# First results copied into the FFN accumulator, x loaded within the first up set, and turns ahead of the narrow block, in a two-layer hybrid decoder trunk

## The chip, the core and the metric

The kernel runs on one core of a Trainium2 chip. Five engines work side by side, each on its own queue of instructions in order: TensorE (PE: matmuls, with weight loads as PEld), VectorE (DVE), ScalarE (ACT), GpSimd (POOL) and SyncE (SP). DMAs are issued from the queues of SP, ACT and POOL. The metric is the time of one execution on the device in microseconds (us). The median of 3 runs of the kernel before is 2119.82 us (2116.66 to 2121.93).

## What is computed

Two layers of a hybrid decoder trunk over 512 tokens of width 1024, in float32. A layer is a mixer (four branches, each lifted and gated, summed, one output projection) and then the part that the change touches, a SwiGLU FFN with an inner width of 2816:

```python
for l in range(DEPTH):                      # 2 layers
    x = x + merged @ w_out                  # the mixer's end
    hf = rmsnorm(x, norm_ffn)
    gate, up = jnp.split(hf @ ffn_w_up, 2, axis=-1)
    x = x + (jax.nn.silu(gate) * up) @ ffn_w_down
```

## The kernel before

**Precision.** Each float32 operand is split in a high half (rounded, `hi`) and the rest (`lo`), and a product is three matmuls, hi·hi, hi·lo, lo·hi (`mm3`, lines 280 to 285). Weights come by DMA on SP's queue into raw buffers; ScalarE writes the high half (`w_hi`, through the helper `A`, so all of ScalarE's work has line 99), VectorE the low half (`w_lo`, line 1099 in `split`, line 236 in `Chunk`).

**Raw buffers.** `raw_tile` (line 1083) hands out buffers of 1 MB: two of `w_raw` and, every third time, the single `w_raw7`. A buffer is used again, in the order in which the program asks for it, only when its last reader is done. The profile names both `w_raw`.

**The FFN.** 2816 inner columns are eleven groups of 256. Ten of them go through a scheme with seven products in place of eight (Strassen's, in Winograd's form), two groups of 256 at a time in an *up set*; the eleventh, group 10, is the *narrow block*, computed plainly in two halves of 128 columns (`up_plain`). The scheme needs sums of blocks of the weights. Those are not computed on an engine: `weight_sums` (line 1104) has GpSimd issue DMAs that copy one block in DRAM and add others to it, each waiting for the one before ("one by one", line 1110). Layer 0's are started early in its mixer, layer 1's at the end of layer 0's FFN (line 1075). They end in DRAM as `up_sums` and `w_sums`, from where SP loads them as raw weights.

**Parts.** Each layer's FFN has three parts (lines 1390 to 1427). A part first makes inner columns, then multiplies them down into the accumulator `acc` (512 tokens by 1024):

- part 0: up set 0 and the narrow block, then `down` over groups 0, 1, 10;
- part 1: up sets 1 and 2, then `down` over groups 2 to 5;
- part 2: up sets 3 and 4, then `down` over groups 6 to 9. In layer 0 the last two groups go through `add_down` (line 1059) instead, which adds `acc` and x as well and writes the next layer's input.

**An up set** (`up_set`, line 1310) has seven products, each of 24 matmuls on one raw buffer, named after the left operand: A11, A12, S2, S1, S3, S4, A22, in this order. Left operands S1 to S4 are sums of quarters of the normalized input `h`, made once per layer by `left_sums` (line 1246), which uses the buffer `acc` as its scratch; S1 alone stands in `h1`, a buffer of the kind `a_hi`/`a_lo`, of which there are four (`N_OPS`); S2 to S4 stand in `hs`. The results, `v` and `u`, are evicted between products. In part 0, `between` (the first half of the narrow block, its result turned and kept in `fy`) stands after A12. S2's weights take the third turn of the raw buffers and S4's the sixth, both `w_raw7` in layer 1.

**Operands.** The inner columns have to be turned (tokens to the free axis) before they can be multiplied down: `turned` (line 1377) makes four 128x128 transposes on TensorE against the identity (line 1380) and a copy on ScalarE. `operands` (line 1147) then makes, from two turned tiles, the quarters and their sums as hi/lo pairs. `pairs_of` (line 1385) does so for an up set's two groups.

**The order in part 0.** After the up set comes the second half of the narrow block (`up_plain(1, ...)`), then `pairs_of` for the set, then two copies on ScalarE that put `h1` into a quarter of `h` that is read no more after the narrow block (this frees the buffer of `h1` for a fourth operand; `where[S1]` then points there), then `acc`, and last the operand of group 10. In layer 0 `acc` is cleared by a memset on GpSimd (line 1405). In layer 1, the last, `acc` starts as x: `x_in` (line 1283) loads half of x from `x_spill` into `w_raw7`, turns 16 tiles on TensorE (line 1289) and copies them into `acc`; it is called twice.

**`down`** (line 1174) does the same scheme on the second matrix, and calls `evict` (line 1412) for each pair of finished banks: VectorE adds the bank to a quarter of `acc`, or subtracts it for the columns `C2` (line 1420). The accumulation in a bank goes on after some of these evictions, so the next matmul into it waits for them. `evict` returns its additions; `split` keeps the low halves of later weights behind them on VectorE (`follow`).

**The planner.** The framework puts the instructions of each engine in an order of its own when the kernel is built: by priority (the written order, raised inside `tc.high_priority`) among those that are ready by its own estimate of times. An instruction that is not ready can so be passed by a later one; on the chip the queue's order is then fixed.

Of the kernel before, what the change touches and what calls it, by code (L numbers as in the profile page):

```python
# [70 lines left out]
def hybrid_trunk(ctx: ExitStack, tc: tile.TileContext, x, mem, positions, norm_mix, w_in, conv_w,  # L71
# [20 lines left out]
    def A(dst, src, func, **kw):  # L92
        name = tables.get(func)
        if name is not None and name != table["set"]:
            load = act.preload_act_table_set(name)
            for u in table["users"]:
                tc.add_manual_dep(load.ins, u.name, order, reason="table set")
            table.update(set=name, load=load.ins, users=[])
        i = act.activation(dst, src, func, **kw)  # L99
        if name is not None:  # L100
            tc.add_manual_dep(i.ins, table["load"].name, order, reason="table set")
            table["users"].append(i.ins)
        return i
# [4 lines left out]
    def at_ps():  # L108
        return pat.tile([P, 512], F32, name="at", bufs=AT_BUFS)
# [1160 lines left out]
    def ffn(l, h, ssq):  # L1270
# [6 lines left out]
        with tc.tile_pool(name="ffn", bufs=1, reuse_waits="tile") as fp:  # L1277
# [21 lines left out]
            def product(bank, o, src, first):  # L1299
                raw = raw_tile(fp).rearrange("p (k n) -> p k n", n=512)  # L1300
                nc.sync.dma_start(raw, src)
                for e in range(2):
                    w = split([(0, 2, raw[:, 2 * e:2 * e + 2, :])])
                    for t, ps in enumerate(bank):
                        for j in range(2):
                            k = 2 * e + j
                            a = [where[o](x, k)[:, t * P:(t + 1) * P] for x in lefts]
                            mm3(ps, a, w[j], first and k == 0, k == 3, not first)

            def up_set(n, between=None):  # L1310

                def block(e, g):
                    c = g * FF + n * 512
                    return w_up[e * 512:(e + 1) * 512, c:c + 512].rearrange("(k p) n -> p k n", p=P)

                sums = wu_dram[l, n]
                b0 = mm_ps()
                ba, bb = [mm_ps(), mm_ps()], [b0, tr_ps()]
                g, v, u = [None] * 2, [None] * 2, [None] * 2

                def now():
                    return tc.high_priority(offset=2 * AHEAD)

                def copies(bank, name, bufs):
                    ts = [fp.tile([P, 512], F32, name=name, bufs=bufs) for _ in bank]
                    with now():
                        for d, ps in zip(ts, bank):
                            A(d, ps, AF.Copy)
                    return ts

                product(ba, A11, block(0, 0), True)
                g = copies(ba, "fg", 2)
                product(bb, A12, block(1, 0), True)
                with now():
                    for t in range(2):
                        dve.tensor_add(g[t], g[t], bb[t])
                        A(g[t], g[t], AF.Silu, scale=r_t[:, t:t + 1])
                if between is not None:
                    between()
                bc = [at_ps(), at_ps()]  # L1340
                product(ba, S2, sums[SUM2], False)
                v = copies(ba, "fu", 4)
                product(bc, S1, sums[SUM1], True)
                u = copies(bc, "fu", 4)
                product(ba, S3, sums[SUM3], False)
                with now():
                    for t in range(2):
                        dve.tensor_add(u[t], u[t], ba[t])
                product(bc, S4, block(1, 1), False)
                with now():  # L1350
                    for t in range(2):
                        dve.tensor_add(v[t], v[t], bc[t])
                        dve.scalar_tensor_tensor(v[t], v[t], nr_t[:, t:t + 1], g[t], op0=OP.mult, op1=OP.mult)
                product(ba, A22, sums[SUM4], False)
                with now():
                    for t in range(2):
                        z = fp.tile([P, 512], F32, name="fg", bufs=2)
                        A(z, ba[t], AF.Silu, scale=r_t[:, 2 + t:3 + t])
                        dve.scalar_tensor_tensor(u[t], u[t], nr_t[:, 2 + t:3 + t], z, op0=OP.mult, op1=OP.mult)
                return v + u  # L1360

            def up_plain(j, bank):

                c = FF // 512 * 512 + j * P
                w = wchunk(w_up.rearrange("(k p) (g c) -> p k g c", p=P, g=2)[:, :, :, c:c + P], KD, 256)
                u = fp.tile([P, NT, P], F32, name="fu", bufs=4)
                for t in range(NT):
                    tokens(w, h, t, bank[t // 2][:, t % 2 * 256:t % 2 * 256 + 256])
                with tc.high_priority(offset=2 * AHEAD):
                    for t in range(NT):  # L1370
                        ps = bank[t // 2][:, t % 2 * 256:t % 2 * 256 + 256]
                        A(u[:, t, :], ps[:, :P], AF.Silu, scale=r_t[:, t:t + 1])
                        dve.scalar_tensor_tensor(u[:, t, :], ps[:, P:], r_t[:, t:t + 1], u[:, t, :],
                                                 op0=OP.mult, op1=OP.mult)
                return [u[:, t, :] for t in range(NT)]

            def turned(us, j, name="fx", bufs=2):
                ps = tr_ps()
                for t in range(NT):
                    pe.transpose(ps[:, t * P:(t + 1) * P], us[t][:, j * P:(j + 1) * P], ident)  # L1380
                g = fp.tile([P, S], F32, name=name, bufs=bufs)
                A(g, ps, AF.Copy)
                return g

            def pairs_of(us, plain):
                return [operands(fp, *(turned(us, 2 * i + j) for j in range(2)), plain, N_OPS) for i in range(2)]

            acc = None
            kept = []
            for part, idx in enumerate(((0, 1, 10), (2, 3, 4, 5), (6, 7, 8, 9))):  # L1390
                if part == 0:
                    us = up_set(0, lambda: kept.append(turned(up_plain(0, [at_ps(), at_ps()]), 0, "fy", 1)))
                    b0 = mm_ps()
                    pls = up_plain(1, [b0, tr_ps()])
                    mm_ps(), mm_ps()
                    ops = pairs_of(us, False)
                    for e in range(2):
                        A(h[e][:, 0:4, HALF:], f(h1[e]), AF.Copy)
                    where[S1] = lambda x, k: x[0][:, k, HALF:]
                    acc = fp.tile([P, NT, D], F32, name="acc")  # L1400
                    if last:
                        x_in(0)
                        x_in(4)
                    else:
                        pool.memset(acc, 0.0)
                    ops.append(operands(fp, kept[0], turned(pls, 0), False, N_OPS))
                else:
                    ops = pairs_of(up_set(2 * part - 1), False)
                    ops += pairs_of(up_set(2 * part), part == 2 and not last)
                final = last and part == 2  # L1410

                def evict(bank, t0, cols, done=False, tail=False):
                    tail = final and tail
                    adds = []
                    with tc.high_priority(offset=2 * AHEAD):
                        for t, ps in enumerate(bank):
                            for w in (slice(0, 256), slice(256, 512)) if tail else (slice(0, 512),):
                                c = slice(cols.start + w.start, cols.start + w.stop)
                                d = acc[:, t0 + t, c]
                                adds.append((dve.tensor_sub if cols is C2 else dve.tensor_add)(d, d, ps[:, w]))  # L1420
                                if final and done:
                                    q = nc.scalar if tail and w.start else nc.sync if t0 or tail else nc.gpsimd
                                    q.dma_start(out[0][(t0 + t) * P:(t0 + t + 1) * P, c], d)
                    return adds

                n = 2 if part == 2 and not last else len(idx)
                down(fp, ffn_w_down[l], wt_dram[l], idx[:n], ops[:n], evict)
# [40 lines left out]
```

## Time and profile before

| | us |
|---|---|
| median of 3 runs (lowest to highest) | 2119.82 (2116.66 to 2121.93) |
| the profiled execution | 2102.95 |
| its span, first to last instruction | 2100.9 |
| PE busy in the span | 2001.4 (95%) |
| DVE busy | 1476.1 (70%) |
| ACT busy | 1190.9 (57%) |
| POOL busy | 229.8 (11%) |
| mean granted clock of PE | 0.979 of full |

In the profile's rows, a row of a timeline has its start, its length, the engine, the line in the kernel, the operation, out<-in, shapes and a count (neighbours of one kind are merged); in brackets stands the idle time of the engine before it and what ended it. A row of waits reads: who <- for whom, total us, times, longest. A row of windows has from:to, length, then for PE, PEld, DVE, ACT and POOL the busy time with the number of instructions, then the granted clock, the busy share of the DMA engines and GB/s. `mm`, `tr` and `at` are the three kinds of PSUM banks. Layer 0's part 0 ends its up set at about 755 us and its narrow block at 766 us of the span; layer 1's at 1789 and 1801 us.

### The profile page before, as it was taken

Reading aid. Unit: us, or ns where it says so; the run is one execution under the profiler, and the core shown is the slowest. Engines: PE = TensorE matmul, PEld = TensorE weight load, DVE = VectorE, ACT = ScalarE, POOL = GpSimd, SP = SyncE. Lnnn points to the kernel's source line nnn. Section 1 sums busy time; section 2 is a strip of 40 time slices with the busy share of each in tenths; the row PEclk is TensorE's granted clock in tenths of the full one; section 3 lists DMA queues with packets and bytes.
Section 4 is the critical chain, followed back from the end, with each engine's and each line's share of the span. In section 5 each row is a group of like instructions: output and inputs, shape, how many; then the busy total and the mean of one; then the engine's idle time right before and its main releaser. Section 6 shows DMA issues by size and latency. Waiting matters only on the chain.

```text
span 2100.9 us, 27510 instructions
## 1 busy us (share of the span) xinstructions
PE 2001.4 (95%) x10240; PEld 1681.0 (80%) x10240; DVE 1476.1 (70%) x2814; ACT 1190.9 (57%) x2100; POOL 229.8 (11%) x264
## 2 busy tenths in 40 slices
PE   8999999999999980999999999999999999799999
PEld 8898987778888860787889889877788788678787
DVE  5768897557776750677677699965678667467777
ACT  7653564766665540455656536567567545446564
POOL 0011111111111112000001111111111111110000
PEclk9999999999999995999999999999999999999999
DMA  7667666657777774555557765666666778795554
GB/s 251 208 151 187 152 175 170 169 132 180 174 188 196 242 197 90 199 182 180 191 185 196 188 169 151 169 154 169 150 181 163 209 208 244 188 285 180 201 190 140
DMA packets 218564, 385.27 MB, mean 183 GB/s; under 512 B 9646, under 2 KB 124928, under 8 KB 212928
## 3 DMA queue, kind: packets, MB, share of 16 engines
q1 hardware_dynamic: 161920, 244.16, 35.1%
q0 software_dynamic: 50368, 126.50, 28.8%
q10 hardware_dynamic: 6144, 12.87, 1.6%
q8 instruction: 80, 1.31, 0.3%
q14 instruction: 52, 0.43, 0.1%
HBM read 368.81 MB, written 140.51 MB: 242 GB/s over the span
## 4 chain that ended last, share of the span: by engine, by line
PE 58%; DMA 34%; issue 3%; DVE 3%; ACT 2%; POOL 0%; SPq 0%; DVEq 0%; POOLq 0%; ACTq 0%
DMA up_sums<-in_ffn_w_up_dram 18%; PE mm L283 15%; PE mm L284 15%; PE mm L285 14%; DMA w_sums<-in_ffn_w_down_dram 7%; DMA up_sums<-up_sums 4%; PE at L285 2%; PE at L284 2%; PE at L283 2%; DMA w_sums<-w_sums 2%; ACT w_hi L99 1%; DVE acc L1420 1%; PE tr L283 1%; PE tr L284 1%; PE tr L285 1%
## 5 line engine op out<-in xcount | busy, mean ns | idle before, releaser
L99 ACT ACTIVATE w_hi<-w_raw 128x1024 fp32r<-128x1024 f32 (+2 forms) x444 | 456.6, 1035 | 376.4 <-PE mm L284 116.7
L283 PE MATMUL mm<-h_hi,w_hi 128*128 128x512 f32 x960 | 378.5, 395 | 2.8 <-ACT w_hi L99 1.7
L284 PE MATMUL mm<-h_lo,w_hi 128*128 128x512 f32 x960 | 378.7, 394 | 0.0
L285 PE MATMUL mm<-h_hi,w_lo 128*128 128x512 f32 x960 | 376.9, 394 | 1.3 <-DVE w_lo L236 1.3
L1099 DVE TENSOR_TENSOR w_lo<-w_raw,w_hi 128x1024 fp32r<-128x1024 f32 (+1 forms) x220 | 256.0, 1174 | 153.4 <-ACT w_hi L99 153.4
L236 DVE TENSOR_TENSOR w_lo<-w_raw,w_hi 128x1024 fp32r<-128x1024 f32 (+1 forms) x224 | 271.8, 1216 | 119.6 <-ACT w_hi L99 119.0
L1109 POOL DMA_DIRECT2D up_sums<-in_ffn_w_up_dram x120 | 121.4, 1011 | 1011.2 <-DMA up_sums<-in_ffn_w_up_dram 526.0
L283 PEld LDWEIGHTS mm<-h_hi,w_hi 128*128 128x128 f32 x960 | 181.3, 189 | 40.5 <-ACT w_hi L99 2.2
L285 PEld LDWEIGHTS mm<-h_hi,w_lo 128*128 128x128 f32 x960 | 181.2, 189 | 37.9 <-DVE w_lo L236 1.9
L284 PEld LDWEIGHTS mm<-h_lo,w_hi 128*128 128x128 f32 x960 | 181.1, 189 | 35.7 <-issue 0.2
L284 PE MATMUL mm<-w_lo,h_hi 128*128 128x256 f32 (+2 forms) x600 | 197.6, 329 | 2.1 <-DVE w_lo L1099 2.1
L285 PE MATMUL mm<-w_hi,h_lo 128*128 128x256 f32 (+2 forms) x600 | 197.4, 329 | 0.0
L283 PE MATMUL mm<-w_hi,h_hi 128*128 128x256 f32 (+2 forms) x600 | 190.1, 329 | 0.0
L284 PEld LDWEIGHTS mm<-w_lo,h_hi 128*128 128x128 f32 x600 | 114.3, 190 | 13.8 <-DVE w_lo L1099 3.9
L283 PEld LDWEIGHTS mm<-w_hi,h_hi 128*128 128x128 f32 x600 | 113.7, 191 | 10.2 <-ACT w_hi L99 0.9
L285 PEld LDWEIGHTS mm<-w_hi,h_lo 128*128 128x128 f32 x600 | 114.3, 191 | 9.2
L283 PE MATMUL mm<-w_hi,a_hi 128*128 128x512 f32 x160 | 59.1, 417 | 65.6 <-DVE acc L1420 56.9
L283 PE MATMUL mm<-y_hi,w_hi 128*128 128x512 f32 x256 | 100.6, 395 | 1.6 <-ACT y_hi L99 1.2
L284 PE MATMUL mm<-y_lo,w_hi 128*128 128x512 f32 x256 | 100.5, 393 | 1.0 <-DVE y_lo L691 1.0
L285 PE MATMUL mm<-y_hi,w_lo 128*128 128x512 f32 x256 | 100.6, 393 | 0.0
L1109 POOL DMA_DIRECT2D w_sums<-in_ffn_w_down_dram x66 | 62.2, 943 | 308.4 <-DMA w_sums<-in_ffn_w_down_dram 181.1
L283 PEld LDWEIGHTS mm<-w_hi,a_hi 128*128 128x128 f32 x160 | 31.2, 196 | 76.8 <-DVE acc L1420 58.1
(451 smaller groups left out, 4300.3 us busy)
## 6 DMA issues: line engine op xcount, KB each, us to landing
w_raw<-in_w_in_dram SPq DMA_DIRECT2D x72, 1024.0 KB, 7.4
up_sums<-in_ffn_w_up_dram POOLq DMA_DIRECT2D x120, 512.0 KB, 6.7
w_raw<-up_sums SPq DMA_DIRECT2D x40, 1024.0 KB, 5.9
w_raw<-in_ffn_w_up_dram SPq DMA_DIRECT2D x30, 1024.0 KB, 5.0
w_sums<-in_ffn_w_down_dram POOLq DMA_DIRECT2D x54, 512.0 KB, 5.8
up_sums<-up_sums POOLq DMA_DIRECT2D x40, 512.0 KB, 5.1
w_raw<-in_w_lift_dram SPq DMA_DIRECT2D x32, 512.0 KB, 4.9
w_raw<-w_sums SPq DMA_DIRECT2D x20, 768.0 KB, 4.1
```

What stands on the lines that cost most here:

```text
L99: i = act.activation(dst, src, func, **kw)
L236: dve.tensor_sub(lo, raw[:, k:e], f(hi))
L283: return [pe.matmul(ps, ah, bh, start=first, stop=False, skip_group_check=more), pe.matmul(ps, ah, bl, start=False, stop=False, skip_group ...
L284: pe.matmul(ps, ah, bl, start=False, stop=False, skip_group_check=more),
L285: pe.matmul(ps, al, bh, start=False, stop=last, skip_group_check=more)]
L1099: follow(dve.tensor_sub(lo[:, k:k + n, :], src, f(hi[:, k:k + n, :])), earlier)
L1109: i = nc.gpsimd.dma_start(dst, src, **kw)
L1420: adds.append((dve.tensor_sub if cols is C2 else dve.tensor_add)(d, d, ps[:, w]))
```

## The change

- The memset on GpSimd is gone. In layer 0, the first time that a quarter of `acc` is reached, `evict` copies the bank into it on ScalarE (scaled by -1 for `C2`) and returns no additions; later evictions add as before. That is 8 of the 16 evictions of part 0 (`touched`).
- `acc` is created, and in layer 1 both halves of x are loaded and turned, by `new_acc`, which `up_set(0)` calls after S3's product and before S4's.
- `pairs_of` for the first set stands before the second half of the narrow block.
- The two copies of `h1` into `h` stand at the start of part 1, ahead of up set 1.

```diff
-            def up_set(n, between=None):
+            def up_set(n, between=None, later=None):
...
                 with now():
                     for t in range(2):
                         dve.tensor_add(u[t], u[t], ba[t])
+                if later is not None:
+                    later()
                 product(bc, S4, block(1, 1), False)
...
+            touched = set()
+
+            def new_acc():
+                nonlocal acc
+                acc = fp.tile([P, NT, D], F32, name="acc")
+                if last:
+                    x_in(0)
+                    x_in(4)
+
             for part, idx in enumerate(((0, 1, 10), (2, 3, 4, 5), (6, 7, 8, 9))):
                 if part == 0:
-                    us = up_set(0, lambda: kept.append(turned(up_plain(0, [at_ps(), at_ps()]), 0, "fy", 1)))
+                    us = up_set(0, lambda: kept.append(turned(up_plain(0, [at_ps(), at_ps()]), 0, "fy", 1)), new_acc)
+                    ops = pairs_of(us, False)
                     b0 = mm_ps()
                     pls = up_plain(1, [b0, tr_ps()])
                     mm_ps(), mm_ps()
-                    ops = pairs_of(us, False)
-                    for e in range(2):
-                        A(h[e][:, 0:4, HALF:], f(h1[e]), AF.Copy)
-                    where[S1] = lambda x, k: x[0][:, k, HALF:]
-                    acc = fp.tile([P, NT, D], F32, name="acc")
-                    if last:
-                        x_in(0)
-                        x_in(4)
-                    else:
-                        pool.memset(acc, 0.0)
                     ops.append(operands(fp, kept[0], turned(pls, 0), False, N_OPS))
                 else:
+                    if part == 1:
+                        for e in range(2):
+                            A(h[e][:, 0:4, HALF:], f(h1[e]), AF.Copy)
+                        where[S1] = lambda x, k: x[0][:, k, HALF:]
...
                     with tc.high_priority(offset=2 * AHEAD):
+                        if not last and (t0, cols.start) not in touched:
+                            touched.add((t0, cols.start))
+                            for t, ps in enumerate(bank):
+                                A(acc[:, t0 + t, cols], ps, AF.Copy, scale=-1.0 if cols is C2 else 1.0)
+                            return adds
```

## The prediction

> **What bounds the kernel now.** I read the page first: the table of slices, the chain that ended last by line, and the groups for a long wait.
>
> ```profile
> PE   8999999999999980999999999999999999799999
> ...
> PEclk9999999999999995999999999999999999999999
> ...
> DMA up_sums<-in_ffn_w_up_dram 18%; PE mm L283 15%; PE mm L284 15%; PE mm L285 14%; DMA w_sums<-in_ffn_w_down_dram 7%; DMA up_sums<-up_sums 4%; PE at L285 2%; PE at L284 2%; PE at L283 2%; DMA w_sums<-w_sums 2%; ACT w_hi L99 1%; DVE acc L1420 1%; PE tr L283 1%; PE tr L284 1%; PE tr L285 1%
> ...
> L283 PE MATMUL mm<-w_hi,a_hi 128*128 128x512 f32 x160 | 59.1, 417 | 65.6 <-DVE acc L1420 56.9
> ```
>
> TensorE works in every slice but one, the sixteenth (788 to 840 us), and there its clock is halved. Yet the chain runs for 18 + 7 + 4 + 2 = 31% of the span, some 651 us, through the DMAs that build the weight sums; they are meant to be background work. One group of matmuls waited 56.9 us for line 1420, the addition into `acc`. Next the waits of PE around that slice, then the rows of GpSimd and VectorE there:
>
> ```profile
> PE mm L283 <- DVE acc L1420: 56.1, 1, 56.1
> PE tr L1380 <- ACT fx L99: 2.5, 1, 2.5
> ...
> 827.44 0.72 POOL L1109 DMA_DIRECT2D w_sums<-in_ffn_w_down_dram  x1 [5.40 <-DMA w_sums<-in_ffn_w_down_dram]
> 832.02 1.13 POOL L1109 DMA_DIRECT2D w_sums<-in_ffn_w_down_dram  x1 [3.86 <-DMA w_sums<-in_ffn_w_down_dram]
> 832.71 3.95 POOL L1405 MEMSET acc<- 128x4096 f32 x1
> ...
> 836.70 1.28 DVE L1420 TENSOR_TENSOR acc<-acc,mm 128x512 f32<-128x512 f32 x2 [56.80 <-POOL acc L1405]
> ```
>
> GpSimd issues the moves of the weight sums one by one, each waiting for the one before. The clearing of `acc` stands in its queue behind layer 0's last move, and starts 0.7 us after that was issued. The 3.95 us of clearing is not the price; its place in the queue is. VectorE, then TensorE, wait for it. The table by windows, with layer 0's junction, the stall, the restart, the stage after; then layer 1's junction and the same stage after it:
>
> ```profile
> 766.50:781.40 14.90, 11.79 (x52) 8.76 (x50) 12.15 (x22) 13.00 (x25) 1.43 (x2) 0.89 0.74 211
> 781.40:837.40 56.00, 0.00 (x0) 0.00 (x0) 0.70 (x2) 0.23 (x1) 13.20 (x11) 0.52 0.49 94
> 837.40:841.50 4.10, 4.06 (x10) 3.19 (x11) 4.10 (x8) 1.04 (x2) 0.00 (x0) 0.50 0.16 20
> 860.00:900.00 40.00, 39.47 (x174) 32.19 (x174) 24.88 (x27) 21.23 (x24) 0.00 (x0) 1.00 0.59 209
> 1801.20:1834.00 32.80, 20.23 (x91) 16.41 (x90) 18.32 (x33) 19.26 (x36) 5.54 (x6) 0.84 0.66 181
> 1853.00:1893.00 40.00, 39.47 (x174) 32.21 (x173) 24.90 (x26) 21.56 (x25) 5.54 (x6) 1.00 0.88 282
> ```
>
> First number: length; second: PE busy; the column after POOL: granted clock. The rest of the FFN is full: 39.47 of 40 us.
>
> **Part 1: the clearing goes, first results are copied.** Removed: 56.0 us of stall in layer 0, and the restart's half clock: 4.1 us at 0.50 is 2.05 us of lost work. What is late next? The first copies of `acc`, now on ScalarE:
>
> ```profile
> 707.76 0.60 ACT L99 ACTIVATE fg<-mm 128x512 f32<-128x512 f32 x1 [0.53 <-PE mm L285]
> ...
> L1420 DVE TENSOR_TENSOR acc<-acc,mm x60: 676/680/689, 836.7 to 2094.6; 128x512 f32<-128x512 f32 x60
> ```
>
> A copy of one bank takes 0.60 us against 0.68 for an addition. Eight additions (5.4 us of VectorE) become eight copies (4.8 us of ScalarE); ScalarE is busy 21.23 of 40 us here and has the room. Queued behind a copy are the high halves of weights (`w_hi`), 1.2 us late for a pair; behind an addition it was the low halves. I book nothing for it; bounds -2 to +2 us.
>
> Without the stall, layer 0's last moves run beside TensorE's work. Layer 1 already does that: its window 1853 to 1893 has GpSimd issuing six moves and 282 GB/s, and PE is busy 39.47 of 40, exactly as in layer 0's window without moves. I book 1 us; bounds 0 to 15 (second rival). Nor does a sum come late:
>
> ```profile
> 1016.70 12.14 SPq L1301 DMA_DIRECT2D w_raw<-up_sums  x3
> ...
> 1051.22 5.76 SPq L1204 DMA_DIRECT2D w_raw<-w_sums  x2
> ```
>
> Layer 0's last sums are read at 1016.70 and 1051.22, some 63 us earlier afterwards, and were issued by 832.02: over 120 us of slack.
>
> **Part 2: turns ahead of the narrow block, and the copy of `h1` moved to the next part.** In the old order ScalarE's queue stands still before the junction:
>
> ```profile
> 1789.78 0.37 PE L284 MATMUL mm<-w_lo,h_hi 128*128 128x256 f32 x1
> 1801.13 0.60 PE L1380 MATMUL tr<-ident,fu 128*128 128x128 f32 x4
> ...
> 1799.77 1.06 ACT L99 ACTIVATE h_hi<-a_hi 128x1024 fp32r<-128x1024 f32 x1 [8.06 <-PE tr L284]
> 1802.62 1.07 ACT L99 ACTIVATE fx<-tr 128x512 f32<-128x512 f32 x2
> 1804.40 0.37 ACT L99 ACTIVATE fu<-mm,rstd_t 128x128 f32<-128x128 f32 x1
> ```
>
> The copy into `h_hi` overwrites what the narrow block reads, so it waits 8.06 us for that block's last matmul, and the block's own silus (1804.40) stand behind it. The turns of the first set come only at 1801.13. Afterwards the set's operands are made under the block's 11.3 us (1789.8 to 1801.1); only the third operand, from the block itself, remains. Its chain: silu and product 0.4 each, turn 0.6, copy 0.5, two pairs of halves, in all about 4 us by my estimate, under the first four half-products, 24 matmuls at 39.47 / 174 = 0.227, 5.4 us. So it is nearly covered; if TensorE meets its turn too soon, 1 to 3 us show. I leave 1.5 us per layer. The moved copies, two of 1.06 us, go where ScalarE has room.
>
> Layer 0's junction holds 14.90 - 11.79 = 3.1 us idle, and at clock 0.89 another 1.6: 4.7, of which 3.2 go.
>
> **Part 3: x within the last layer's first set.** Layer 1's junction: 32.80 - 20.23 = 12.6 us idle, and at clock 0.84 another 5.2: 17.8. Its waits and the sync queue's rows:
>
> ```profile
> PE tr L1289 <- DMA w_raw<-x_spill: 4.6, 1, 4.6
> PE mm L283 <- ACT w_hi L99: 4.6, 1, 4.6
> PE mm L283 <- DVE fu L1373: 1.8, 1, 1.8
> PE tr L1380 <- ACT fx L99: 1.5, 1, 1.5
> ...
> 1764.07 0.38 SPq L1301 DMA_DIRECT2D w_raw<-in_ffn_w_up_dram  x1
> 1778.13 0.34 SPq L1285 DMA_DIRECT2D w_raw<-x_spill  x1
> 1813.35 0.32 SPq L1285 DMA_DIRECT2D w_raw<-x_spill  x1
> 1822.02 0.38 SPq L1195 DMA_DIRECT2D w_raw<-in_ffn_w_down_dram  x1
> ...
> 1818.62 3.37 PE L1289 MATMUL tr<-ident,w_raw 128*128 128x128 f32 x16 [4.61 <-DMA w_raw<-x_spill]
> 1822.19 0.48 PE L283 MATMUL tr<-w_hi,a_hi 128*128 128x512 f32 x1
> ```
>
> Both 4.6 us waits come from one buffer, `w_raw7`: the second half of x waits in it for the first (1813.35 to 1818.62, 5.3 us), the third operand's weights for the second. Both go with the move. But the buffer then serves, in order, the set's S2 weights, x twice, its S4 weights. The latter were issued at 1764.07, when S2's split ended (the row at 1762.83). Now they come two links later, each a load of 5.3 us and the turns of 16 tiles. A split and a group of eight turns took:
>
> ```profile
> 1761.85 1.06 ACT L99 ACTIVATE w_hi<-w_raw 128x1024 fp32r<-128x1024 f32 x1
> 1762.83 1.22 DVE L1099 TENSOR_TENSOR w_lo<-w_raw,w_hi 128x1024 fp32r<-128x1024 f32 x1
> ...
> 1812.28 1.04 PE L1289 MATMUL tr<-ident,w_raw 128*128 128x128 f32 x8
> ...
> 1778.02 1.28 DVE L1348 TENSOR_TENSOR fu<-fu,mm 128x512 f32<-128x512 f32 x2
> ```
>
> so a link is 5.3 + 2.1 = 7.4 us, and S4's weights land at 1764.1 + 14.8 + 5.3 = 1784.2, split by 1786.5 (1.06 + 1.22). S3 ends at 1778 (its addition starts at 1778.02), the turns of x add 4.2 us: wait 4.3 us. If the turns come only after S3 (TensorE is full until then), the links start there: 1778 + 2.1 + 5.3 + 2.1 + 5.3 + 2.3 = 1795.1, a wait of 12.9. Against it, TensorE has A22's product (24 matmuls, 5.4 us) and the narrow block's 11.3 us, which need neither S4 nor this buffer: together 16.7. If the planner draws them forward, all is covered; behind S4 on the queue, nothing is. Bounds 0 and 13; the planner did send later loads past the waiting x at 1813.35, so I take 5. At the same place a rule speaks against the change. The row at 1818.62 shows 16 turns in 3.2 us, begun at half clock after an idle time, and the matmul behind them (0.48, with the pipe's start) at full speed again: turns alone brought the clock back. By the Trainium skill, "TensorE: Matmul & The Clock Gate", Part 4: PE-mode transpose, the clock gate does not count turns as work in the same way; x's 32 turns, 4.2 us, would then let the clock fall and the sum would be an estimated 2 us smaller. Here the trace disagrees, so the sum stays.
>
> **Sum.** 56.0 + 2.05 + 4.7 + 17.8 = 80.6 us; less 3.0 (two third operands), 5 (S4), 1 (moves): 71.6. From the profiled execution's 2102.95: 2031.4. The median of the shown runs, 2119.82, lies 16.9 us above it. If that excess is spread or constant, it stays: **2048**.
>
> **Rivals.**
> 1. *The excess lies in the stall.* The chain goes for 651 us through moves; 2.6% slower moves are 16.9 us more stall, and leave with it: 2031. For it: nothing else in the chain is so exposed to the memory. Against it: the stall is seen in one execution alone, and a fixed cost around the program would look the same.
> 2. *Transfers are the next bound.* All moves and loads share the DMA engines: 0.49 of them busy in the stall, 0.59 in the stage after, 1.08 together. The excess 0.08 of 56 us is 4.5 us; at 94 + 209 = 303 GB/s against 282 seen, 4; with bursts, 15: 2062. The windows of layer 1 speak against. The Trainium skill ("DMA: Bandwidth & Descriptors", Issuing engines are not separate DMA queues) says the same, that queues of different engines interleave on the same 16 DMA engines; the trace's 39.47 of 40 us at 0.88 shows it harmless.
> 3. *S4's weights hold the last layer:* 13 us instead of 5, then the clock at half for 4 us, and the set's operands late past the narrow block (6 us): 16 us more, 2064.
> 4. *It doesn't do what it says:* the copies into `acc` still meet a wait on GpSimd's queue: 2119. Against: nothing else of this part is on that queue.
> 5. *Slower: the pause was TensorE's rest.* If, working without it, the granted clock falls, each 1% costs some 20 us of 2031; it decides against the change from 3.5% (71.6 / 2031), and at 0.95 it takes 2048 to 2150. Against it: the clock stands at 1.00 in both 40 us windows, long after any pause.
>
> **How the numbers follow.** Forecast (2036 to 2058) 0.55; rival 1: 0.2; 2: 0.05; 3: 0.15; 4: 0.02; 5: 0.03. The range 2026 to 2064 holds the first two, rival 2 and most of 3: its lower end is rival 1 with S4 covered, its upper end rival 3. About 0.3% (6 us) is what a measurement tells from no change. Faster 0.95, same 0.02, slower 0.03.
>
> **What would show it.** No MEMSET on GpSimd in the sixteenth slice; PE without a wait over 5 us between 766 and 860; the moves after 781 beside a busy PE. In layer 1 no wait for `x_spill` at the junction; the wait to look for is a matmul of S4 for `w_hi`, and where A22 stands. I would be wrong if PE waits for DMA in the 60 us after the junction, or if layer 1's span from its first up set to the next shrinks by less than 3 us.

## The result and the profile after

| | before | after |
|---|---|---|
| median of 4 runs each (us) | 2120.42 (2116.66 to 2121.93) | 2039.84 (2036.11 to 2043.2) |
| ratio, 95% interval | | 0.962 [0.960, 0.964] |
| profiled execution (us) | 2102.95 | 2040.42 |
| its span (us) | 2100.9 | 2038.7 |

The change takes 80.6 us from the median, but only 62.2 us from the span of the two profiled executions. The time came out 8 us under the forecast of 2048 and inside the range. That closeness is in part luck. Two errors of the forecast work against each other: the median lost more in layer 0 than it counted on, and almost nothing in layer 1.

First the page of the kernel after: TensorE's busy tenths, the granted clock, and the chain that ended last by line.

```profile
PE   8999999999999999999999999999999998999999
...
PEclk9899999999999999999999999999999998999999
...
PE mm L283 23%; PE mm L284 23%; PE mm L285 23%; PE at L285 3%; PE at L284 3%; PE at L283 3%; PE tr L283 1%; PE tr L284 1%; PE tr L285 1%; ACT w_hi L99 1%; PE tr L746 1%; PE tr L740 1%; PE tr L1382 1%; PE at L714 1%; PE at L715 1%; DMA w_raw<-in_w_in_dram 1%
```

The hole in the sixteenth slice is gone, and with it the moves of the weight sums, which had 31% of the chain. One dip is left behind the first slice, in the 34th (1682 to 1733 us), and there the clock dips too.

Now layer 0 in windows of the kernel after: from:to, length, busy time of PE, PEld, DVE, ACT, POOL with counts, granted clock, DMA share, GB/s.

```profile
766.00:782.00 16.00, 14.61 (x78) 12.15 (x76) 10.85 (x19) 11.34 (x20) 2.33 (x2) 1.00 0.79 191
782.00:802.00 20.00, 19.10 (x80) 14.25 (x78) 13.71 (x17) 11.12 (x16) 2.60 (x3) 1.00 0.85 271
802.00:840.00 38.00, 37.72 (x166) 31.26 (x167) 24.02 (x26) 19.83 (x23) 5.56 (x6) 1.00 0.95 273
```

The junction holds 1.4 us of idle time, and behind it the moves run beside a TensorE that is busy 37.72 of 38 us, though the DMA engines are busy 0.95 of the time. How much layer 0 gained is read from one and the same load of the second up set of part 1, on SP's queue, in the kernel before and in the kernel after:

```profile
884.60 5.82 SPq L1301 DMA_DIRECT2D w_raw<-in_ffn_w_up_dram  x2
```

```profile
823.54 5.82 SPq L1301 DMA_DIRECT2D w_raw<-in_ffn_w_up_dram  x2
```

884.60 - 823.54 = 61.1 us, and the whole span gained 62.2. So layer 1, for which 11.3 us were forecast, gave about 1. The stage in which the dip lies, the last layer's part 0, goes from the first load of its first up set to the first load of the next one. In the kernel before:

```profile
1713.07 10.96 SPq L1301 DMA_DIRECT2D w_raw<-in_ffn_w_up_dram  x2
...
1840.57 7.50 SPq L1301 DMA_DIRECT2D w_raw<-in_ffn_w_up_dram  x2
```

In the kernel after, with the loads that take turns in `w_raw7` between them (L1285 is x, 1727.98 is S4's weights):

```profile
1652.50 10.96 SPq L1301 DMA_DIRECT2D w_raw<-in_ffn_w_up_dram  x2
...
1702.20 0.32 SPq L1285 DMA_DIRECT2D w_raw<-x_spill  x1
...
1719.38 0.34 SPq L1285 DMA_DIRECT2D w_raw<-x_spill  x1
1727.98 0.37 SPq L1301 DMA_DIRECT2D w_raw<-in_ffn_w_up_dram  x1
...
1778.56 7.82 SPq L1301 DMA_DIRECT2D w_raw<-in_ffn_w_up_dram  x2
```

The stage took 127.5 us before and takes 126.1 now. TensorE's rows there, and its waits in that stretch (who <- for whom, us in total, times, longest):

```profile
1712.39 0.71 PE L1289 MATMUL tr<-ident,w_raw 128*128 128x128 f32 x5
...
1718.76 0.60 PE L1289 MATMUL tr<-ident,w_raw 128*128 128x128 f32 x4
1724.30 3.65 PE L1289 MATMUL tr<-ident,w_raw 128*128 128x128 f32 x16 [4.95 <-DMA w_raw<-x_spill]
1734.31 1.22 PE L283 MATMUL at<-w_hi,hs_hi 128*128 128x512 f32 x2 [6.37 <-ACT w_hi L99]
```

```profile
PE at L283 <- ACT w_hi L99: 6.4, 1, 6.4
PE tr L1289 <- DMA w_raw<-x_spill: 4.9, 1, 4.9
PE mm L284 <- DVE w_lo L1099: 2.2, 2, 1.7
```

Read the two views side by side and the chain of the single buffer stands there. The first half of x is turned among S3's matmuls, from 1712.39 on; its last turns end at 1719.4; at 1719.38 SP issues the second half; TensorE stands 4.95 us for it, turns it, and at 1727.98 S4's weights are issued; TensorE stands 6.37 us for those. 11.3 us idle, and the windows show what the clock adds:

```profile
1724.30:1727.95 3.65, 3.65 (x16) 3.24 (x16) 0.00 (x0) 1.79 (x3) 0.01 (x1) 0.50 0.60 107
1727.95:1734.31 6.36, 0.00 (x0) 0.00 (x0) 0.02 (x1) 1.70 (x3) 1.13 (x1) 0.50 0.84 227
1734.31:1739.15 4.84, 4.80 (x11) 3.31 (x12) 3.48 (x3) 1.84 (x2) 0.72 (x1) 0.50 0.43 91
...
1747.80:1780.00 32.20, 32.17 (x197) 28.38 (x196) 25.04 (x40) 21.28 (x34) 4.42 (x5) 1.00 0.75 205
```

3.65 and 4.84 us of work at clock 0.50 are some 4 us lost, by estimate: 15.5 us in all at this place. The junction itself, the last window, has become what the change wanted: 32.17 of 32.20 us busy, where it was 20.23 of 32.80. The gain there and the new loss nearly cancel.

### The profile page after: what moved, and what is told of

The parts are those of the page before. It is cut to its first block, busy times and chain, and to the rows that moved or that the text cites. A ratio compares the mean times of both kernels' runs of the same rounds, so it can differ in the third digit from the quotient of the medians.

```text
span 2038.7 us, 27492 instructions
## 1 busy us (share of the span) xinstructions
PE 1996.6 (98%) x10240; PEld 1677.8 (82%) x10240; DVE 1472.9 (72%) x2806; ACT 1194.8 (59%) x2108; POOL 226.6 (11%) x263
## 4 chain that ended last, share of the span: by engine, by line
PE 91%; DVE 4%; DMA 3%; ACT 2%; issue 0%; SPq 0%; DVEq 0%; ACTq 0%
PE mm L283 23%; PE mm L284 23%; PE mm L285 23%; PE at L285 3%; PE at L284 3%; PE at L283 3%; PE tr L283 1%; PE tr L284 1%; PE tr L285 1%; ACT w_hi L99 1%; PE tr L746 1%; PE tr L740 1%; PE tr L1382 1%; PE at L714 1%; PE at L715 1%; DMA w_raw<-in_w_in_dram 1%
## 5 line engine op out<-in xcount | busy, mean ns | idle before, releaser
L285 PE MATMUL mm<-h_hi,w_lo 128*128 128x512 f32 x960 | 376.2, 393 | 1.3 <-DVE w_lo L236 1.3
L1109 POOL DMA_DIRECT2D up_sums<-in_ffn_w_up_dram x120 | 121.5, 1012 | 945.4 <-DMA up_sums<-in_ffn_w_up_dram 541.9
L285 PEld LDWEIGHTS mm<-h_hi,w_lo 128*128 128x128 f32 x960 | 180.8, 188 | 37.8 <-DVE w_lo L236 1.9
L285 PE MATMUL mm<-w_hi,h_lo 128*128 128x256 f32 (+2 forms) x600 | 198.2, 331 | 0.0
L285 PEld LDWEIGHTS mm<-w_hi,h_lo 128*128 128x128 f32 x600 | 115.1, 192 | 9.2
L285 PE MATMUL mm<-y_hi,w_lo 128*128 128x512 f32 x256 | 100.5, 393 | 0.0
L99 ACT ACTIVATE prob<-prob,small 128x128 f32<-128x128 f32 (+3 forms) x128 | 68.9, 554 | 17.6 <-DVE small L729 12.6
L544 DVE TENSOR_TENSOR gate<-mm,rstd 128x512 f32<-128x512 f32 x64 | 44.0, 688 | 32.2 <-PE mm L285 32.0
```

The costliest lines, as they stand in the source:

```text
L285: pe.matmul(ps, al, bh, start=False, stop=last, skip_group_check=more)]
L544: dve.tensor_mul(g, ps, r_b)
L1109: i = nc.gpsimd.dma_start(dst, src, **kw)
```

## The experiments

Theory A: the 16.9 us by which the median lies above the profiled execution belong to the stall (rival 1 of the prediction). Theory C: in the last layer the loss is the place of S4's weights behind both halves of x in `w_raw7`. The stage of a kernel below means the time between the two loads on SP's queue read above. Kernels e1 to e3 ran side by side on one chip (before: 2121.67 us, median of 7), and so did e4 to e7 (before: 2122.18, median of 11).

**e0: the kernel before, once more.**

> The kernel before, unchanged, profiled a second time. Theory A (the 16.9 us by which the median of before lay above its profiled execution are stall: the moves of the weight sums go slower in most executions): the span is longer than 2100.9, TensorE's one long wait for the addition into acc is longer by the same amount (about 70 us at a span of 2116), and the rest of the span is as long as it was, within 3 us. Theory B (the excess is spread over the work, or a fixed cost outside the span): the wait is 56 us again, and a longer span is longer everywhere.

It took 2123.67 us (one execution), with a span of 2121.6. The first of TensorE's waits between 700 and 900 us, then the clearing:

```profile
PE mm L283 <- DVE acc L1420: 77.4, 1, 77.4
```

```profile
854.28 3.95 POOL L1405 MEMSET acc<- 128x4096 f32 x1
```

The span is 20.7 us longer than in the first profile and the wait 21.3 us longer (77.4 for 56.1). The clearing takes the same 3.95 us; it starts 21.6 us later, since the chain of moves ahead of it was slower. Theory A holds: what differs between the spans of these two executions lies in the stall. The moves were slow before it, though. The chain starts at 113.4 and at 113.5 us; the same move, the thirteenth from its end, is issued at 764.27 us in the first profile and at 787.82 in e0, and from there to the last move it takes 67.8 and 65.8 us. So the delay was gathered beside the mixer and the first up set, and TensorE paid for it in the stall.

**e1: copies of the first results alone.**

```diff
-                    else:
-                        pool.memset(acc, 0.0)
...
+                        if not last and (t0, cols.start) not in touched:
+                            touched.add((t0, cols.start))
+                            for t, ps in enumerate(bank):
+                                A(acc[:, t0 + t, cols], ps, AF.Copy, scale=-1.0 if cols is C2 else 1.0)
+                            return adds
```

> Before with part 1 alone: no memset, first results copied; turns, h1 and x stay where they were. Theory A (the memset's place in GpSimd's queue is the price): the wait of 56 us or more is gone, nothing of GpSimd takes its place, the time falls by 58 us from the profiled execution's 2103 and by up to 75 from the median 2120, so 2042 to 2048, as much as the whole change gave or within 6 us of it. Rival (the change as a whole is needed, since without the earlier turns the junction is next): gain under 45 us.

2044.61 us (2040.47 to 2046.95), ratio 0.964 [0.959, 0.970]: 77 us less than before. This one edit brings nearly all that the whole change brings. The stage in layer 1 takes 129.8 us, no shorter than before.

**e2: the clearing stays, on VectorE's queue.**

```diff
-                        pool.memset(acc, 0.0)
+                        dve.memset(acc, 0.0)
```

> Before with one word changed: the same memset, on VectorE. Theory A: the stall goes as in the copies, since VectorE's queue holds no moves; the clearing itself costs 2 to 4 us on VectorE at the junction, of which 0 to 4 show: 2042 to 2052. Rival (writing acc by copies in place of additions is what helps): 2110 or more.

2050.19 us (2046.78 to 2052.18), ratio 0.967 [0.962, 0.972]. The instruction is still there, and over 70 us are gone: the place in GpSimd's queue was the price. On VectorE it takes 3.47 us and starts at 730.01 us, within the up set and not at the junction. The median lies 5.6 us above e1's; the two profiled executions, with spans of 2044.7 and 2045.2 us, don't show that difference, and its cause stays open.

**e3: the changed kernel with x at its old place**, behind the narrow block.

```diff
                 acc = fp.tile([P, NT, D], F32, name="acc")
-                if last:
-                    x_in(0)
-                    x_in(4)
...
                     mm_ps(), mm_ps()
+                    if last:
+                        x_in(0)
+                        x_in(4)
                     ops.append(operands(fp, kept[0], turned(pls, 0), False, N_OPS))
```

> The changed kernel, but x loaded and turned at its old place, after the narrow block. Theory C (in the changed kernel the last layer's S4 product pays back in the up set what the earlier turns save at the junction): the S4 wait of 6.4 us and the wait for x of 4.9 us in the up set go, both 4.6 us waits at the junction come back, and the time is within 5 us of the changed kernel. Rival D (moving x is a gain of its own): 10 us or more slower than the changed kernel.

2034.51 us (2031.7 to 2036.94), ratio 0.960 [0.954, 0.966]. Without the third part the kernel is as fast or faster, not slower: 5.3 us below the changed kernel's median above, taken in another set of runs; that is a little more than the 5 us that theory C allowed. TensorE's waits between 1680 and 1800 us here:

```profile
PE tr L1289 <- DMA w_raw<-x_spill: 5.9, 1, 5.9
PE mm L283 <- ACT w_hi L99: 3.5, 1, 3.5
PE mm L284 <- DVE w_lo L1099: 1.6, 2, 1.1
```

These are the junction's waits of the kernel before; none is S4's. The waits for `fx` and `fu`, 1.5 and 1.8 us before, are gone: that is what the turns ahead of the narrow block bring. The stage takes 121.5 us, 8.3 less than in e1. (From e1 to e3 the copies of `h1` move as well; the two weren't parted.)

**e4: another buffer for S4**, by moving the turn of the raw buffers on by one in the last layer. `w_raw7` then serves A12, S3 and both halves of x; S4 and A22 use the pair.

```diff
-    def raw_tile(fp, turn=[0]):
+    turn = [0]
+    def raw_tile(fp):
...
+            turn[0] += last
             acc = None
```

> The changed kernel, with the turn of the raw buffers shifted by one in the last layer's up set: the single w_raw7 then serves A12, S3 and both halves of x, and S4's and A22's weights go through the pair of w_raw. Theory C (the changed kernel loses some 15 us in the last layer because S4's weights stand behind both halves of x in that one buffer): the wait of PE for w_hi of S4's first matmul (6.4 us) and the wait for x_spill (4.9 us) fall under 2 us each, and the time is 2022 to 2030 us. Rival E (the loss is x's loads and 32 turns themselves, wherever their buffer is): the time stays at 2035 to 2042 us.

2034.66 us (2031.0 to 2038.15), 9.4 less than the changed kernel beside it (e5), between the ranges of the two theories; the stage takes 123.1. Waits of TensorE from 1670 to 1800 us (lines are two higher):

```profile
PE mm L283 <- ACT w_hi L99: 5.1, 1, 5.1
...
PE at L283 <- ACT w_hi L99: 0.7, 1, 0.7
...
PE tr L1291 <- DMA w_raw<-x_spill: 0.5, 1, 0.5
```

Both waits that theory C names are down to 0.7 and 0.5 us. But there is a new one of 5.1 us, and it is not in the same place:

```profile
1683.84 0.80 PE L283 MATMUL mm<-w_hi,h_hi 128*128 128x512 f32 x1 [5.06 <-ACT w_hi L99]
```

It is near the start of the up set: shifted by one, A12's weights now stand in `w_raw7`, and SP issues them 24.6 us after the set's first (1672.42 for 1647.80), where it was some 10.6 in the changed kernel. SP's queue waits there twice: 12.4 us for VectorE's split of A11's weights (L1101), to issue S2's load (1671.99), which stands ahead of A12's; then 0.2 us for a matmul of L285, the last of which for the mixer's output starts at 1672.17. Which of the two would have held A12's load alone is not shown. A shift of a ring moves every load in it.

**e5: the changed kernel again.**

> The changed kernel once more, beside the others of this set. All theories: 2036 to 2043 us, with the waits of 4 to 7 us for x_spill and for S4's w_hi in the last layer again.

2044.06 us (2039.95 to 2045.82), ratio 0.963 [0.960, 0.967], 1 us above the range expected; waits of 5.8 us for x and 6.4 for S4's weights; the stage takes 127.7 us.

**e6: copies, and x moved, without the turns ahead.** e1 with `new_acc` as in the changed kernel, `pairs_of` and the `h1` copies at their old place.

```diff
-                    us = up_set(0, lambda: kept.append(...))
+                    us = up_set(0, lambda: kept.append(...), new_acc)
...
-                    acc = fp.tile([P, NT, D], F32, name="acc")
-                    if last:
-                        x_in(0)
-                        x_in(4)
```

> The kernel before with copies of the first results and x within the last layer's up set, but the turns and the h1 copies at their old place. It completes a table of two by two: copies alone 2044.6, with turns ahead 2034.5, with both turns ahead and x moved 2039.8. If the two moves add up independently: 2044.6 + 5.3 = 2050 (2046 to 2053). Theory C (x moved costs some 15 us at S4 and saves what the junction lost to x; the junction without turns ahead loses more to x than the one with them): less than that sum, 2043 to 2047. A time under 2040 would speak against both.

2051.27 us (2046.66 to 2051.57), ratio 0.967 [0.963, 0.971], as the sum of two independent moves gives it (2050); theory C's finer guess of 2043 to 2047 missed. The waits:

```profile
PE at L283 <- ACT w_hi L99: 9.0, 1, 9.0
PE tr L1289 <- DMA w_raw<-x_spill: 7.0, 1, 7.0
PE tr L1382 <- ACT fx L99: 2.3, 1, 2.3
```

The same two waits, larger, and the operands' wait besides. The stage takes 136.2 us, 6.4 more than in e1: moved alone to that place, x is a loss.

**e7: x asked for behind S4's product** instead of ahead of it, all else as in the changed kernel.

```diff
-                if later is not None:
-                    later()
                 product(bc, S4, block(1, 1), False)
...
+                if later is not None:
+                    later()
                 product(ba, A22, sums[SUM4], False)
```

> The changed kernel, with both halves of x asked for after S4's product and before A22's, in place of before S4's; the buffers' turn is as in the changed kernel, so S4's weights come first in w_raw7, then x twice, then the weights of the third operand. Theory C: no wait for S4's w_hi, x covered by A22 and the narrow block (16.7 us against two links of 7.4): 2023 to 2031 us. Rival E: 2035 to 2042 us. If the third operand's weights come late instead, a wait for w_hi at the junction of 3 to 5 us: 2028 to 2036 us.

2027.84 us (2023.83 to 2035.62), ratio 0.957 [0.953, 0.960]: 16 us below the changed kernel beside it, with no overlap of the two sets of runs, and the fastest version of this study. TensorE's waits between 1670 and 1800 us, and SP's loads:

```profile
PE mm L284 <- DVE w_lo L1099: 2.3, 2, 1.7
PE tr L1289 <- DMA w_raw<-x_spill: 2.0, 1, 2.0
```

```profile
1699.71 0.38 SPq L1301 DMA_DIRECT2D w_raw<-in_ffn_w_up_dram  x1
...
1713.76 0.57 SPq L1285 DMA_DIRECT2D w_raw<-x_spill  x1
...
1727.86 0.34 SPq L1285 DMA_DIRECT2D w_raw<-x_spill  x1
1736.46 0.38 SPq L1195 DMA_DIRECT2D w_raw<-in_ffn_w_down_dram  x1
```

The links are the same; only their order differs. S4's weights (1699.71) come first, x's two links lie under A22 and the narrow block, and the third operand's weights still come in time. S4's wait of 6.4 us is gone, and the stage takes 114.5 us, 13.0 less than before. That is the gain that the change meant to have there. TensorE is busy for 111.33 us of the stage, at granted clock 1.00; for the same matmuls it was busy for 114.81 in the kernel before (clock 0.96) and for 114.68 in the changed one (0.93). The differences, 3.5 and 3.4 us, are what half clock cost there, by estimate.

**e8: x's turns six times over**, on e3: each of x's 32 turns is made six times into the same place.

```diff
-                    for t in range(NT):
+                    for t in [0, 1, 2, 3] * 6:
                         pe.transpose(...)
```

> The kernel of e3 (x at its old place), with each of x's 32 turns made six times over in its bank, so that the result is the same and TensorE turns for long with no other matmul between: 48 turns in two rows, and 96 on end behind the wait for x's second half. In the changed kernel 16 turns behind such a wait took 3.65 us, 0.218 us each, half clock, but an idle time stood behind them. Theory T (turns bring the clock back and hold it, as I read the row at 1818.62 of before): the 96 turns take some 3.5 us at 0.218 each and the rest, 80, at 0.123, together 13 us, the matmuls behind them are at full speed, and the 160 more turns cost 20 us: 2052 to 2058 us. Rival G (turns do not count as work for the clock): the 96 turns stay at 0.218 each, 21 us, and some 10 matmuls behind them come at half speed: 30 us more than e3 or above, 2063 to 2070 us.

2051.05 us, one execution on another chip, 1 us under the range of theory T. Rows of TensorE, then windows over them:

```profile
1739.85 5.40 PE L1289 MATMUL tr<-ident,w_raw 128*128 128x128 f32 x48
...
1758.61 12.21 PE L1289 MATMUL tr<-ident,w_raw 128*128 128x128 f32 x96 [3.97 <-DMA w_raw<-x_spill]
...
1771.01 0.48 PE L283 MATMUL tr<-w_hi,a_hi 128*128 128x512 f32 x1
```

```profile
1739.85:1745.25 5.40, 5.40 (x51) 5.40 (x50) 3.13 (x5) 3.67 (x7) 1.13 (x1) 1.00 0.48 149
...
1758.61:1762.20 3.59, 3.59 (x19) 3.59 (x20) 0.00 (x0) 0.00 (x0) 0.50 (x1) 0.56 0.30 54
1762.20:1770.60 8.40, 8.40 (x79) 8.40 (x78) 0.00 (x0) 1.79 (x3) 1.35 (x2) 1.00 0.53 106
```

48 turns leave the clock at 1.00. Behind an idle 3.97 us the first 3.6 us of turns run at 0.56, and then, with nothing but turns between, at 1.00. These turns bring the clock back and hold it, as the prediction read it from a row of 3.37 us (its text has 3.2) at 1818.62. The Trainium skill, "TensorE: Matmul & The Clock Gate", Part 4: PE-mode transpose, has it that such a transpose does not count as work for the clock in the same way; these rows disagree for float32 turns of 128x128.

## Why the prediction was right, and where it was wrong

**The clearing and its stall: right, and of two sizes.** The mechanism is shown by e1 and e2. The size, 56.0 us, was that of one execution; in e0 it is 77.4. The prediction kept the excess of the median (16.9 us) as something that stays; e0 (one execution) and the 77 us that e1 takes from the median speak for stall that left with the clearing. Rival 1, at 0.2, had this right: the chain of moves is what was slow. Why its pace changes, no run shows.

**Layer 0's sum: right.** Forecast 56.0 + 2.05 + 3.2 - 1 = 60.3, measured 61.1. The 1.5 us left for the third operand are 1.4 in the first window. Rival 2 (transfers) is out: 0.95 of the DMA engines' time, and TensorE at 37.72 of 38. Rival 5 is out: granted clock 1.00 there.

**Layer 1's junction: right, somewhat too large.** 17.8 us were to go, less a rest of 1.5; the window 1747.80 to 1780 is full, and e3 and e7 show its two parts apart: turns ahead (with the copies of `h1`) 8.3 us of stage (129.8 to 121.5), x at a good place 7.0 more (121.5 to 114.5). Against the kernel before, e7's stage is 13.0 us shorter, not 16.3: 2.0 us of waiting for x are left, and the 5.2 us for the clock were reckoned over the whole window, idle time too, where the stage shows 3.5.

**S4's wait: the term that was mis-sized.** "So I take 5" stood between bounds of 0 and 13; it measured 11.3 us idle and some 4 us of half clock. The upper bound's own arithmetic (two links begun when S3 ends) nearly gave it. What failed was the reason for the low value: that A22's product and the narrow block, 16.7 us that need neither S4 nor `w_raw7`, could be drawn forward. Two rows of the changed kernel, ScalarE's split and TensorE's first matmul of A22, show where they stood:

```profile
1733.20 2.95 ACT L99 ACTIVATE w_hi<-w_raw 128x1024 fp32r<-128x1024 f32 x3 [4.62 <-DMA w_raw<-in_ffn_w_up_dram]
...
1740.07 0.63 PE L283 MATMUL mm<-w_hi,h_hi 128*128 128x512 f32 x2
```

A22's raw weights were asked for at 1705.81, 22 us ahead of S4's. But no high half is made between 1711.8 and 1733.20; then, with S4's weights there, ScalarE makes three in a row. A product has two, so by the program's order these are S4's two and A22's first. A22's matmuls start only at 1740.07, behind S4's first at 1734.31. So the 16.7 us were not ready work: A22's split stood behind S4's on ScalarE's queue, and the narrow block's came later still. The prediction asked only which buffer this work needs, and left out the queue that prepares its weights. e7, which puts both links of x behind S4's load, shortens the stage to 114.5 us. By the prediction's own test, a stage shrunk by under 3 us, its third part was wrong (1.4). Rival 3 had the mechanism; of its 16 us beyond the 5, the 6 us for late operands did not come.

**The sum put right:** 2031.4 + 9.9 (layer 1's 1.4 for 11.3) - 0.8 (layer 0) = 2040.5, where the profiled execution took 2040.42. This puts the measured changes of two stages in place of the forecast ones; it shows that the rest of the span stayed as it was, and no more.

**The copies of `h1`: no effect seen.** They still run right behind the narrow block in the changed kernel (767.3 us); the planner put them there again, and they were not tried alone.

## What to carry to other kernels

Ask of every instruction what stands ahead of it in its queue: 3.95 us of clearing cost 56 to 77 us because of a chain of transfers ahead of it; with the same clearing on VectorE's queue the median came within 6 us of the one without it. When a load moves up into a single buffer, write down the buffer's order of use and see who now comes last; the same two links cost some 15 us ahead of S4 and 2.0 us of waiting behind it. Before an estimate counts on other work to fill a wait, follow that work back through every queue that prepares it: here the matmuls of A22 were free of the buffer, and the split of their weights was not free of the load that waited.

## What the runs showed of the hardware

The chain of moves has no fixed pace. Between the kernel before and e0, with the same instructions, its end moved by 21.6 us, and the span by 20.7. The runs of the kernel before spread from 2105.3 to 2130.9 us on one chip, those of e1 from 2040.5 to 2047.0. The delay of e0 was gathered while TensorE worked. The chain's last stretch, from one and the same move to the last one, took 67.8 us in the kernel before and 65.8 in e0, mostly beside an idle TensorE (DMA engines busy for 0.47 of 796 to 833 us in the first). Without the stall it runs beside work and loads and is slower: 80.3 us in the changed kernel (0.87 to 0.90 between 784 and 856), 84.7 in e1, 91.0 in e3. The first move of the stretch, in the kernel before, in e0 and in the changed kernel:

```profile
764.27 1.14 POOL L1109 DMA_DIRECT2D up_sums<-in_ffn_w_up_dram  x1 [5.48 <-DMA up_sums<-in_ffn_w_up_dram]
```

```profile
787.82 1.14 POOL L1109 DMA_DIRECT2D up_sums<-in_ffn_w_up_dram  x1 [5.61 <-DMA up_sums<-in_ffn_w_up_dram]
```

```profile
775.06 1.14 POOL L1109 DMA_DIRECT2D up_sums<-in_ffn_w_up_dram  x1 [6.04 <-DMA up_sums<-in_ffn_w_up_dram]
```

The last ones are issued at 832.02, 853.58 and 855.34 us. Behind the junction of the changed kernel TensorE waits for none of these moves.
